# First norm of the decoder trunk: x is turned unscaled, the root of the mean square is multiplied in later, and x and the first weight tiles load on two queues

## The chip, the cores and the metric

The kernel runs on one core of a Trainium2 chip. The metric is device time in microseconds (us) of one execution; lower is better. The engines named below are TensorE (PE; PEld is its weight load), VectorE (DVE), ScalarE (ACT), GpSimd (POOL) and SyncE (SP). SP issues nearly all DMAs; ACT can issue DMAs too, from its own instruction stream.

## The reference

A trunk of two layers over 256 tokens of width 1024, in fp32. Only the first sub-layer is touched:

```
def rms_norm(x, g):
    y = x * rsqrt(mean(x * x, axis=-1) + 1e-6)
    return y * g
...
def short_conv_mixer(h, w_in, conv_w, w_out):
    b_gate, c_gate, z = split(h @ w_in, 3, axis=-1)      # w_in is 1024 x 3072
    u = c_gate * z
    u_conv = causal depthwise convolution of u, width 3
    return (b_gate * u_conv) @ w_out
...
x = x + short_conv_mixer(rms_norm(x, norm_mix[0]), conv_w_in, conv_w, conv_w_out)
x = x + peer_ffn(rms_norm(x, norm_ffn[0]), ...)          # then attention, and a second peer_ffn
```

The root of the mean square is one number per token. It multiplies all three parts of `h @ w_in`, so it can be applied to a product instead of to x.

## The kernel before

All products run on TensorE as three products of two parts each (a high part and a rest): high weight by high x, low weight by high x, high weight by low x. Weights come as a stream of numbered **items** of 128 x 1024 fp32 (512 KB). Items 0 to 23 are `conv_w_in` (four DMAs of 128 KB each), items 24 to 31 `conv_w_out`, then the peer layer follows. Three buffers `raw`, `hi`, `lo` go round, so item n uses buffer n mod 3.

- `split_to(n)` (L162 on): ACT copies `raw` to `hi` (L171), then DVE or POOL computes `lo = raw - hi` (L176). Items 0, 1, 2 and 25 of this layer have their `lo` on POOL (`on_pool`), the others on DVE. Item 0's `lo` is made in two halves (`halved`).
- `issue()` (L129 on) issues the DMAs of item n+3 as soon as item n is split.
- `next_item(mm, budget)` emits the split of item n+2, then the products of item n, then calls `run_side(budget)`, which emits queued side work (`add(cost, f)`) until the budget is spent; `pause` ends a round. So the order in which each engine works is the order in which the Python code emits; every engine takes its instructions strictly in that order.
- `mm_wstat(banks, b)` (L472): one item of `conv_w_in`, 24 products of 128 x 256. Items 0 to 7 go to the PSUM banks `lo4` (the c gate), 8 to 15 to `hi4` (z), 16 to 23 to `lo4` again (the b gate). I call these the first, second and third group.
- `norm_in()` computes the first norm: squares on ACT (L334), the root in small DVE steps (`begun`, `mean`, `root`), a multiplication by root and gain (`scaled`, L367), turning by TensorE (`turned`, L372) and splitting into high part `XH` (L377) and rest `XL` (L382). The gain row is spread over the partitions by TensorE (`spread_gain`, L276).
- After the first group ACT copies `lo4` to `cT` (L583). In the third group, DVE and ACT compute the convolution as side work: u (L588, DVE), first tap (L592, ACT), two more taps (L594, DVE). After item 23, DVE multiplies the b gate by the convolution (L610) and the result is split into `XH` and `XL` (L611, L605) for `conv_w_out`.
- Before all that, `warm(n)` issues n products on the identity to raise the granted clock, and `preload()` has ACT load its table.

Of the kernel before, what the change touches and what calls it, by code (L numbers as in the profile page):

```python
# [22 lines left out]
D = 1024  # L23
# [15 lines left out]
def trunk_kernel(ctx: ExitStack, tc, x, norm_mix, norm_ffn, conv_w_in, conv_w, conv_w_out,  # L39
# [89 lines left out]
    def issue():  # L129
        while state["dma"] < NI and released(state["dma"] - 3):  # L130
# [15 lines left out]
            elif isinstance(items[n][1], list):  # L146
                for q in (0, 2, 1, 3):
                    sp.dma_start(r[32 * q:32 * q + 32], items[n][1][q])
            else:
                sp.dma_start(r, items[n][1])  # L150
# [11 lines left out]
    def split_to(n):  # L162
        while state["split"] <= min(n, NI - 1):
# [6 lines left out]
            else:  # L170
                act.activation(HI[m % 3], src, AF.Copy)  # L171
# [88 lines left out]
    def load_x(i, h):  # L260
        c = slice(h * 512, h * 512 + 512)
        sp.dma_start(x_in[:, i * D + h * 512:i * D + h * 512 + 512], x[0, i * 128:(i + 1) * 128, c])
# [10 lines left out]
    def spread_gain(gb):  # L273

        for h in range(2):
            pe.matmul(gb[h], half_row, GN[0:1].rearrange("p (q c j) -> p c q j", q=4, j=32)[:, 4 * h:4 * h + 4],  # L276
                      start=True, stop=True)

    for i in range(2):
        for h in range(2):  # L280
            load_x(i, h)
        if i == 0:
            sp.dma_start(GN[0:1], norm_mix[0:1])
# [8 lines left out]
    half_row = scratch(0, 128)[0:1]  # L292
    dve.memset(half_row, -0.5)
# [7 lines left out]
    warm(WARM)  # L301
    spread_gain(hi4[2:4])
# [21 lines left out]
    def residual(bank, i, h):  # L324

        v = XT[i].rearrange("p (c q j) -> p c q j", q=4, j=32)[:, :, 2 * h:2 * h + 2]
        if bank is None:
            bank = x_in[:, i * D + h * 512:i * D + h * 512 + 512]
            dve.tensor_copy(v, bank.rearrange("p (q c j) -> p c q j", q=2, j=32))
            v = bank  # L330
        else:
            dve.tensor_tensor(v, bank.rearrange("p (q c j) -> p c q j", q=2, j=32), v, op=OP.add)
            v = XT[i].rearrange("p (c r) -> p c r", r=128)[:, :, 64 * h:64 * h + 64]
        act.activation(junk[:, 0:512] if len(v.shape) == 2 else junk[:, 0:512].rearrange("p (c r) -> p c r", r=64),  # L334
                       v, AF.Square, accum_out=ssq[:, 2 * i + h:2 * i + h + 1])
# [16 lines left out]
    def rms(banks):  # L352
        bk = banks or [None] * 4
        residual(bk[0], 0, 0)
        begun(0)
        residual(bk[1], 0, 1)
        mean(0)
        residual(bk[2], 1, 0)
# [26 lines left out]

    def norm_in():

        scaled, turned, first, parted = norm_parts(hi4, hi4[2:4])
# [854 lines left out]
```

## Time and profile before

| | us |
|---|---|
| median of 3 runs | 1823.19 (1821.16 to 1823.33) |
| the profiled execution | 1822.49 |
| its span | 1820.7 |
| TensorE busy in the span | 1797.7 |

The span is the time from the first to the last instruction on the core in the profile; the execution's own time has 1.8 us around it. A stretch in which TensorE has no gap can only become shorter by fewer products.

### The profile page before, as it was taken

The page shows a single profiled execution, that of the slowest core. Times are in us where ns is not written, and L with a number is a line of the kernel's source. Part 1 is how long each engine was busy: PE and PEld are TensorE (multiplying, and loading weights), DVE is VectorE, ACT ScalarE, POOL GpSimd, SP SyncE. Part 2 cuts the span into 40 slices and gives each one's busy share as a digit, 9 for nine tenths or more (in the row PEclk, how much of TensorE's full clock was granted, in tenths as well). Part 3 has the DMA queues.
Part 4 walks back from the last instruction along what each step waited for, and adds up shares of the span by engine and source line. Part 5 has one row for each costly group of instructions (what it writes and reads, how often), then busy time and mean ns, then how long its engine had stood idle before and what let it go on. Part 6 is the DMA issues. An engine that isn't in the chain of part 4 may idle for free.

```text
span 1820.7 us, 32357 instructions
## 1 busy us (share of the span) xinstructions
PE 1797.7 (99%) x11985; PEld 1573.6 (86%) x11985; DVE 1353.9 (74%) x2183; ACT 894.6 (49%) x1109; POOL 710.7 (39%) x549
## 2 busy tenths in 40 slices
PE   9999999999999999999999999999999999999998
PEld 8979999988888888888788799999888888888886
DVE  4748888788888887555567487887888898875555
ACT  5455445555454444544454554545455544445443
POOL 1048899978820000000200388999888300000000
PEclk9999999999999999999999999999999999999999
DMA  7566655665555555655562675556565555556564
GB/s 210 154 194 188 183 163 168 175 178 168 172 161 183 166 173 183 227 193 194 163 184 86 174 205 169 166 169 183 165 172 167 160 185 174 174 174 228 191 194 138
DMA packets 204581, 321.15 MB, mean 176 GB/s; under 512 B 26221, under 2 KB 157317, under 8 KB 203910
## 3 DMA queue, kind: packets, MB, share of 16 engines
q1 hardware_dynamic: 202006, 312.33, 56.2%
q10 hardware_dynamic: 2416, 6.75, 1.1%
q8 instruction: 94, 1.54, 0.4%
q14 instruction: 65, 0.53, 0.1%
HBM read 315.83 MB, written 3.15 MB: 175 GB/s over the span
## 4 chain that ended last, share of the span: by engine, by line
PE 90%; DVE 4%; DMA 2%; ACT 1%; POOL 1%; issue 1%; SPq 0%; DVEq 0%; ACTq 0%; POOLq 0%
PE psum L485 41%; PE psum L878 13%; PE psum L884 12%; PE psum L880 5%; PE psum L881 5%; PE psum L1085 3%; PE psum L472 3%; PE psum L518 2%; DVE big L215 1%; POOL lo L176 1%; DVE tr L157 1%; PE psum L916 1%; DVE lo L176 1%; DMA raw<-in_conv_w_out_dram 1%; ACT hi L171 1%
## 5 line engine op out<-in xcount | busy, mean ns | idle before, releaser
L176 POOL TENSOR_TENSOR lo<-tr,hi 128x512 fp32r<-128x512 f32 x496 | 652.3, 1348 | 109.4 <-ACT hi L171 104.8
L176 DVE TENSOR_TENSOR lo<-raw,hi 128x1024 fp32r<-128x1024 f32 x316 | 388.1, 1229 | 259.1 <-ACT hi L171 253.1
L171 ACT ACTIVATE hi<-raw 128x1024 fp32r<-128x1024 f32 x331 | 349.7, 1060 | 448.4 <-PE psum L485 365.4
L485 PE MATMUL psum<-hi,x 128*128 128x512 f32 x2208 | 553.0, 392 | 0.7 <-ACT hi L171 0.7
L485 PEld LDWEIGHTS psum<-hi,x 128*128 128x128 f32 x2208 | 409.0, 188 | 82.6 <-ACT hi L171 1.1
L157 DVE STREAM_TRANSPOSE tr<-raw 128x1024 f32<-128x1024 f32 x256 | 316.0, 1234 | 64.2 <-POOL lo L176 38.2
L171 ACT ACTIVATE hi<-tr 128x1024 fp32r<-128x1024 f32 x256 | 270.3, 1058 | 128.4 <-DVE tr L157 113.5
L884 PE MATMUL psum<-x,lo 128*128 128x256 f32 x2048 | 292.0, 283 | 6.2 <-POOL lo L176 6.2
L485 PE MATMUL psum<-lo,x 128*128 128x512 f32 x1104 | 295.2, 389 | 0.4 <-POOL lo L176 0.4
L884 PEld LDWEIGHTS psum<-x,lo 128*128 128x128 f32 x2048 | 273.6, 191 | 18.6 <-POOL lo L176 8.6
L176 POOL TENSOR_TENSOR lo<-raw,hi 128x512 fp32r<-128x512 f32 (+1 forms) x27 | 49.1, 1848 | 609.5 <-ACT hi L171 557.3
L878 PE MATMUL psum<-x,hi 128*128 128x512 f32 x1024 | 263.6, 398 | 0.0
L880 PE MATMUL psum<-x,hi 128*128 128x256 f32 x1024 | 252.7, 284 | 0.8 <-ACT hi L171 0.8
L881 PE MATMUL psum<-x,hi 128*128 128x256 f32 x1024 | 251.1, 283 | 0.0
L485 PEld LDWEIGHTS psum<-lo,x 128*128 128x128 f32 x1104 | 207.1, 188 | 43.9 <-POOL lo L176 0.8
L878 PEld LDWEIGHTS psum<-x,hi 128*128 128x128 f32 x1024 | 183.6, 189 | 33.3
L880 PEld LDWEIGHTS psum<-x,hi 128*128 128x128 f32 x1024 | 196.3, 192 | 1.5 <-ACT hi L171 1.2
L881 PEld LDWEIGHTS psum<-x,hi 128*128 128x128 f32 x1024 | 196.4, 192 | 0.2
L1185 POOL TENSOR_TENSOR big<-xbuf,big 128x256 f32<-128x256 f32 x2 | 1.4, 732 | 383.4 <-DVE rstd L348 383.4
L1070 DVE TENSOR_TENSOR xbuf<-psum,eT 128x1536 f16<-128x1536 f16 x128 | 119.9, 937 | 10.1 <-PE psum L1085 10.1
L1040 ACT ACTIVATE big<-psum 128x512 f32<-128x512 f32 x64 | 38.2, 597 | 125.6 <-PE psum L884 125.6
L1022 ACT ACTIVATE big<-psum 128x512 f32<-128x512 f32 x64 | 38.1, 596 | 115.6 <-PE psum L884 115.5
(164 smaller groups left out, 1573.4 us busy)
## 6 DMA issues: line engine op xcount, KB each, us to landing
raw<-in_peer_u_dram SPq DMA_DIRECT2D x1024, 128.0 KB, 3.0
raw<-in_peer_v_dram SPq DMA_DIRECT2D x256, 512.0 KB, 4.2
raw<-in_conv_w_in_dram SPq DMA_DIRECT2D x96, 128.0 KB, 2.6
raw<-in_attn_w_qkv_dram SPq DMA_DIRECT2D x96, 128.0 KB, 2.7
raw<-in_peer_w_q_dram SPq DMA_DIRECT2D x64, 128.0 KB, 2.9
raw<-in_conv_w_out_dram SPq DMA_DIRECT2D x8, 512.0 KB, 4.2
raw<-in_attn_w_o_dram SPq DMA_DIRECT2D x8, 512.0 KB, 3.7
x_dram<-xbuf ACTq DMA_DIRECT2D x2, 1024.0 KB, 4.8
```

Source lines behind the costliest of these rows:

```text
L157: dve.transpose(TR[m % 3].rearrange("p b (g i) -> p g b i", g=4), RAW[m % 3].rearrange("p (g m) -> p g m", m=256))
L171: act.activation(HI[m % 3], src, AF.Copy)
L176: eng.tensor_sub(LO[m % 3][:, c], src[:, c], HI[m % 3][:, c])
L472: pe.matmul(banks[c // 2][:, (c % 2) * 256:(c % 2) * 256 + 256], w[:, c * 128:c * 128 + 128], xx[:, b], start=(b == 0 and p == 0 and c % 2 ...
L485: pe.matmul(banks[j], x[:, j // 2 * 128:j // 2 * 128 + 128], w[:, j % 2 * 512:j % 2 * 512 + 512], start=(first and p == 0), stop=(last and ...
L878: pe.matmul(o, w, X2[:, b], start=(b == 0), stop=False, skip_group_check=True)
L880: pe.matmul(o, w, XH[:, b], start=(b == 0), stop=False)
L881: pe.matmul(o, w, XL[:, b], start=False, stop=False)
L884: pe.matmul(o[:, 0:256], lo[:, b * 128:b * 128 + 128], XH[:, b], start=False, stop=(b == 7), skip_group_check=(o.shape[-1] == 512))
L1040: act.activation(A[:, k - 1:k + 1], halves(k, 1), AF.Copy)
L1070: dve.tensor_tensor(HOT[s % 2].rearrange("p b (r k) t -> p b r k t", r=3), numbers[:, None, None].to_broadcast([128, TOK // 2, 3, 64, 2]), ...
L1085: pe.matmul(o, pairs[:, t // 2, :, t % 2], OHG[s % 2][:, a, t // 2, :, t % 2], start=(a == 0), stop=(a == 1))
```

## The change

The order of the work in the first sub-layer, not its result, is changed:

- x is loaded in other halves (128 columns of each quarter, so 512 bytes in a row where it was 2 KB): the first halves on ACT's queue, the second on SP's. Item 1's four DMAs go on ACT's queue too. The norm weight comes as 8 rows of 128 and is turned by TensorE into `gT`, one column per chunk.
- x is put in order by DVE (`kept`), turned as it is by TensorE and multiplied by the gain as it is split (`chunk`: ACT writes `XH`, DVE `XL`), chunk by chunk; chunks 0 to 3 ahead of item 0's products, 4 to 7 after item 1's.
- Item 0's `hi` is made in two halves, and its products run in the order high-high, high-low, low-high. Only item 0 is split ahead (before: items 0 and 1).
- Squares, mean and root become side work of items 2 to 4. `factors(i)` puts the root on a diagonal and TensorE multiplies it by ones, after items 4 and 5; `row` makes from that `R` (the root, minus one half included, in a row for all partitions) and `R2` (its square).
- `cT` is made by DVE as `lo4` times `R2` (before: copied by ACT). In the third group u and the first taps (`gate`) are queued one step ahead of the other taps (`taps`), and each pair of chunks is multiplied by `R` (`normed`, new).
- The loads of the second norm's gain and of the peer keys on ACT's queue move from before item 0's products into the second group.

The diff, cut to its core:

```
+    gr8 = scratch(7 * D + 128, 128)[0:8]
+    sp.dma_start(gr8.rearrange("c (q j) -> c q j", q=4), norm_mix[0].rearrange("(q c j) -> c q j", q=4, j=32))
     for i in range(2):
-        for h in range(2):
-            load_x(i, h)
-        if i == 0:
-            sp.dma_start(GN[0:1], norm_mix[0:1])
+        load_x(act, i, 0)
+    issue(1)
+    for i in range(2):
+        load_x(sp, i, 1)
     issue()
...
+    def chunk(c):
+        bk = hi4[c // 2][:, c % 2 * 256:c % 2 * 256 + 256]
+        for i in range(2):
+            pe.transpose(bk[:, i * 128:i * 128 + 128], XT[i][:, c * 128:c * 128 + 128], ident)
+        act.activation(XH[:, c], bk, AF.Copy, scale=gT[:, c:c + 1])
+        dve.scalar_tensor_tensor(XL[:, c], bk, gT[:, c:c + 1], XH[:, c], op0=OP.mult, op1=OP.subtract)
...
     def norm_in():
...
+        for i in range(2):
+            kept(i, 0)
+        chunk(0)
         split_to(0)
+        for c in (1, 2, 3):
+            chunk(c)
+        warm(2)
+        def factors(i):
+            dg = scratch(i * 128, 128)
+            dve.tensor_scalar(dg, ident, rstd[:, i:i + 1], -0.5, op0=OP.mult, op1=OP.mult)
+            pe.matmul(hi4[0][:, i * 128:i * 128 + 128], ones, dg, start=True, stop=True)
+        def row():
+            dve.tensor_copy(R, hi4[0][:, 0:256])
+            dve.tensor_tensor(R2, R, hi4[0][:, 0:256], op=OP.mult)
+        pause(2)
+        for i in range(2):
+            for h in range(2):
+                add(0.3, squares, i, h)
+            add(0.2, begun, i)
+            add(0.2, mean, i)
+        pause()
+        for i in range(2):
+            add(0.6, root, i)
+            add(0.2, factors, i)
+        pause()
+        add(0.6, row)
...
-            next_item(mm_wstat(lo4, b), 1.0)
+            next_item(mm_wstat(lo4, b), 1.5)
+            if b == 0:
+                for i in range(2):
+                    kept(i, 1)
+            if b == 1:
+                for c in range(4, 8):
+                    chunk(c)
...
-                    act.activation(uc[:, c], uT[:, c, 0:256], AF.Copy, scale=cwT[:, 0, c:c + 1])
-                    for k in (1, 2):
-                        dve.scalar_tensor_tensor(uc[:, c], uT[:, c, k:k + 256], cwT[:, k, c:c + 1], uc[:, c],
-                                                 op0=OP.mult, op1=OP.add)
-                add(0.9, f)
+        def normed(j):
+            s = slice(2 * j, 2 * j + 2)
+            dve.tensor_tensor(uc[:, s], uc[:, s], R[:, None].to_broadcast([128, 2, 256]), op=OP.mult)
+        add(0.6, gate, 0)
+        for j in range(4):
+            if j < 3:
+                add(0.6, gate, j + 1)
+            for k in (1, 2):
+                add(0.9, taps, j, k)
+            add(0.6, normed, j)
...
-            next_item(mm_wstat(lo4, b), 2.4, b < 7)
+            next_item(mm_wstat(lo4, b), 2.5, b < 7)
```

Three places show how the engines' orders move. Lines of the changed kernel are numbered anew: L171 becomes L173, L176 L178, L472 L486, L588 L615, L592 L617, L594 L621, L610 L648.

The first place is the start of the program on ACT, in the changed kernel; a wait named DMAHW is one for an earlier DMA (DMAHW0 is that of x's first part, DMAHW2 that of item 0's first quarter).

```order
L265 DMA big<-in_x_dram 128x4x128 x2
L148 DMA raw_67<-in_conv_w_in_dram 32x1024 x2
L148 DMA raw_67<-in_conv_w_in_dram 32x1024 [waits DMAHW0_49]
L148 DMA raw_67<-in_conv_w_in_dram 32x1024 [waits DMAHW2_49]
L255 ACT_TABLE_LOAD
L255 ACTIVATE idle<-one 128x1 [waits DVE_49]
L256 ACTIVATE idle<-one 128x1 [waits Activation_49]
L387 ACTIVATE x_78<-psum,gT 128x256 [waits PE_49]
L173 ACTIVATE hi_72<-raw_66 128x512 [waits DMAHW7_49,DMAHW5_49,DMAHW1_49]
L173 ACTIVATE hi_72<-raw_66 128x512
```

Before, the table load was ACT's first instruction; now six DMA issues stand ahead of it, two of which wait for landings.

On POOL the same place reads, in the changed kernel:

```order
L178 TENSOR_TENSOR lo_75<-raw_66,hi_72 128x512 x2
L314 IOTA iota_t 128x128
L590 MEMSET big 128x8x2
L178 TENSOR_TENSOR lo_76<-raw_67,hi_73 128x1024
L178 TENSOR_TENSOR lo_77<-raw_68,hi_74 128x1024
```

Before, the iota and the memset (L312, L576) stood behind the `lo` of item 1; now they stand ahead of it.

The second place is the end of item 4 on PE in the changed kernel (item 4 uses hi_73 and lo_76, item 5 hi_74); L416 is the product in `factors`.

```order
L486 MATMUL psum<-x_78,lo_76 128x256 [waits DVE_49]
L486 MATMUL psum<-x_78,lo_76 128x256 x7
L486 MATMUL psum<-x_78,hi_73 128x256 x8
L416 MATMUL psum<-big 128x128 [waits DVE_49]
L486 MATMUL psum<-x_78,hi_74 128x256 [waits Activation_49]
L486 MATMUL psum<-x_78,hi_74 128x256 x7
```

What it waits for on DVE (L415, behind the split of item 6, which is lo_75 here):

```order
L178 TENSOR_TENSOR lo_77<-raw_68,hi_74 128x1024
L335 TENSOR_SCALAR part<-ssq 128x1
L339 TENSOR_SCALAR var<-ssq,part 128x1
L178 TENSOR_TENSOR lo_75<-raw_66,hi_72 128x1024
L345 RECIPROCAL rstd<-newt 128x1
L346 TENSOR_SCALAR newt<-rstd,var 128x1
L347 TENSOR_SCALAR rstd<-newt,rstd 128x1
L415 TENSOR_SCALAR big<-ident,rstd 128x128
```

Before, nothing stood between items 4 and 5 on PE; now a product does that needs the `lo` of item 6 and the root.

The third place is the third group on DVE, from the split of item 18 on: first before, then in the changed kernel (L626 is `normed`).

```order
L176 TENSOR_TENSOR lo_75<-raw_66,hi_72 128x1024
L588 TENSOR_TENSOR big<-big,psum 128x2x256
L594 SCALAR_TENSOR_TENSOR big<-big,cwT 128x256 x2
L176 TENSOR_TENSOR lo_76<-raw_67,hi_73 128x1024
L594 SCALAR_TENSOR_TENSOR big<-big,cwT 128x256 x2
L588 TENSOR_TENSOR big<-big,psum 128x2x256
L594 SCALAR_TENSOR_TENSOR big<-big,cwT 128x256 x2
L176 TENSOR_TENSOR lo_77<-raw_68,hi_74 128x1024
```

```order
L178 TENSOR_TENSOR lo_75<-raw_66,hi_72 128x1024
L615 TENSOR_TENSOR big<-big,psum 128x2x256 x2
L621 SCALAR_TENSOR_TENSOR big<-big,cwT 128x256 x2
L178 TENSOR_TENSOR lo_76<-raw_67,hi_73 128x1024
L621 SCALAR_TENSOR_TENSOR big<-big,cwT 128x256 x2
L626 TENSOR_TENSOR big<-big 128x512
L615 TENSOR_TENSOR big<-big,psum 128x2x256
L178 TENSOR_TENSOR lo_77<-raw_68,hi_74 128x1024
L621 SCALAR_TENSOR_TENSOR big<-big,cwT 128x256 x4
L626 TENSOR_TENSOR big<-big 128x512
L615 TENSOR_TENSOR big<-big,psum 128x2x256
L178 TENSOR_TENSOR lo_75<-raw_66,hi_72 128x1024
```

Before, each L588 had two taps between it and the next split; now each L615 of items 19 on stands right ahead of a split. On ACT the two first taps that follow from an L615 (L617) stand ahead of the `hi` of the next item in every round; before, one of the two stood ahead of it and the other behind.

## Rows read from the trace of the kernel before

**Rows 1.** The page: busy time by engine; chain that ended last, by engine.

```profile
PE 1797.7 (99%) x11985; PEld 1573.6 (86%) x11985; DVE 1353.9 (74%) x2183; ACT 894.6 (49%) x1109; POOL 710.7 (39%) x549
...
PE 90%; DVE 4%; DMA 2%; ACT 1%; POOL 1%; issue 1%; SPq 0%; DVEq 0%; ACTq 0%; POOLq 0%
```

**Rows 2.** Chain of waits up to 150 us: start us, us, what.

```profile
1.19 0.42 SPq L262
...
2.02 4.46 DMA big<-in_x_dram
...
12.22 3.14 PE psum L472 x24
15.36 0.87 PE psum L372 x8
...
19.27 40.52 PE psum L472 x336
...
85.75 1.06 ACT hi L171
```

**Rows 3.** Timeline, 0 to 30 us: start us, us, engine, line, operation, [idle before].

```profile
0.74 1.28 ACT L253 ACT_TABLE_LOAD   x1 [0.74 <-PEq L1230]
...
2.04 0.20 ACT L253 ACTIVATE idle<-one 128x1 f32<-128x1 f32 x1
...
3.80 0.43 DVE L329 COPY xbuf<-big 128x512 f32<-128x512 f32 x1 [2.34 <-DMA big<-in_x_dram]
...
10.97 4.89 POOL L176 TENSOR_TENSOR lo<-raw,hi 128x512 fp32r<-128x512 f32 x3 [9.90 <-DMA raw<-in_conv_w_in_dram]
...
15.81 0.84 POOL L312 IOTA iota_t<- 128x128 f16 x1
...
16.67 2.41 POOL L176 TENSOR_TENSOR lo<-raw,hi 128x1024 fp32r<-128x1024 f32 x1
```

**Rows 4.** Stretches: PE, PEld, DVE, ACT, POOL busy us, granted clock, DMA share, GB/s.

```profile
6.00:8.00 2.00, 1.24 (x3) 0.18 (x1) 1.58 (x5) 1.14 (x3) 0.00 (x0) 0.91 1.05 284
8.00:10.00 2.00, 1.80 (x9) 1.49 (x10) 1.62 (x7) 1.15 (x5) 0.00 (x0) 0.50 1.04 283
...
36.00:48.00 12.00, 12.00 (x103) 12.00 (x102) 5.11 (x5) 5.32 (x6) 0.00 (x0) 1.00 0.62 192
...
78.00:84.00 6.00, 5.96 (x47) 5.62 (x46) 5.92 (x10) 2.52 (x4) 0.00 (x0) 1.00 0.67 201
```

**Rows 5.** Groups by line and shape up to 125 us: busy us, mean ns | idle before.

```profile
L171 ACT ACTIVATE hi<-raw 128x1024 fp32r<-128x1024 f32 x38 | 39.6, 1054 | 34.7 <-PE psum L472 19.4 <-DMA raw<-in_conv_w_out_dram 7.1 <-DMA raw<-in_conv_w_in_dram 5.3
L176 DVE TENSOR_TENSOR lo<-raw,hi 128x1024 fp32r<-128x1024 f32 x30 | 37.9, 1270 | 34.8 <-ACT hi L171 32.3 <-DMA raw<-in_conv_w_in_dram 2.1 <-PE psum L485 0.3
...
L594 DVE SCALAR_TENSOR_TENSOR big<-big,cwT 128x256 f32<-128x256 f32 x16 | 7.7, 484 | 2.6 <-ACT big L592 2.3
...
L334 ACT ACTIVATE big<-big 128x512 f32<-128x512 f32 x4 | 2.5, 630 | 2.5 <-DMA big<-in_x_dram 2.4
...
L276 PE MATMUL psum<-big 1*128 1x512 f32 x4 | 2.0, 613 | 0.0
```

**Rows 6.** Timelines of ACT and of DVE in the third group.

```profile
59.81 1.06 ACT L171 ACTIVATE hi<-raw 128x1024 fp32r<-128x1024 f32 x1 [1.82 <-PE psum L472]
62.76 0.51 ACT L592 ACTIVATE big<-big,cwT 128x256 f32<-128x256 f32 x1 [1.89 <-DVE big L588]
63.18 1.04 ACT L171 ACTIVATE hi<-raw 128x1024 fp32r<-128x1024 f32 x1
...
60.90 1.23 DVE L176 TENSOR_TENSOR lo<-raw,hi 128x1024 fp32r<-128x1024 f32 x1 [1.65 <-ACT hi L171]
62.05 0.68 DVE L588 TENSOR_TENSOR big<-big,psum 128x512 f32<-128x512 f32 x1
63.30 1.01 DVE L594 SCALAR_TENSOR_TENSOR big<-big,cwT 128x256 f32<-128x256 f32 x2 [0.58 <-ACT big L592]
...
81.39 1.31 DVE L610 TENSOR_TENSOR psum<-big,psum 128x512 f32<-128x512 f32 x2
```

More of the change, by code (lines that the diff above doesn't have):

```diff
@@ L127, in released, with issue @@
         return n < 0 or n < state["split"] or (is_u(n) and n < state["tr"])
-    def issue():
-        while state["dma"] < NI and released(state["dma"] - 3):
+    def issue(end=NI):
+        while state["dma"] < end and released(state["dma"] - 3):
             n = state["dma"]
@@ L170, in split_to @@
             else:
-                act.activation(HI[m % 3], src, AF.Copy)
+                for c in (range(0, 1024, 512) if m == 0 else (0,)):
+                    w = slice(c, c + (512 if m == 0 else 1024))
+                    act.activation(HI[m % 3][:, w], src[:, w], AF.Copy)
             eng = pool if (is_u(m) or m in on_pool) and m not in on_dve else dve
@@ L291, in trunk_kernel @@
     dve.tensor_scalar(ident, jp, 0.0, None, op0=OP.is_equal)
-    half_row = scratch(0, 128)[0:1]
-    dve.memset(half_row, -0.5)
+    ones = scratch(256, 128)
+    dve.memset(ones, 1.0)
     i16 = ident.bitcast(BF16)
@@ L299, in warm @@
             pe.matmul(B[0][:, 0:256], i16[:, 0:128], i16, start=True, stop=True)
-    warm(WARM)
-    spread_gain(hi4[2:4])
+    warm(WARM - 8)
+    gT = sb.tile([128, 8], F32, name="gT")
+    pe.transpose(lo4[3][:, 0:8], gr8, ident[0:8, 0:8])
+    dve.tensor_copy(gT, lo4[3][:, 0:8])
+    warm(6)
     def load_keys(l):
@@ L469, in f @@
                 order = [(c, p) for c in range(8) for p in range(3)]
+            elif b == 0:
+                order = [(c, p) for p in (0, 2, 1) for c in range(8)]
             for c, p in order:
@@ L576, in conv_mixer @@
         pool.memset(uT[:, :, 0:2], 0.0)
-        load_gain(norm_ffn, 0)
-        load_keys(0)
         for b in range(8):
-            next_item(mm_wstat(lo4, b), 1.0)
+            next_item(mm_wstat(lo4, b), 1.5)
[5 more added lines that the diff above has]
+                    chunk(c)
         drain_side()
-        for j in range(4):
-            act.activation(cT[:, 2 * j:2 * j + 2].rearrange("p c t -> p (c t)"), lo4[j], AF.Copy)
@@ new lines, in conv_mixer, with gate, taps @@
+        pause()
+        add(0.0, load_gain, norm_ffn, 0)
+        add(0.0, load_keys, 0)
+        for b in range(8):
+            next_item(mm_wstat(hi4, b), 1.5)
+        drain_side()
+        def gate(j):
+            s = slice(2 * j, 2 * j + 2)
+            dve.tensor_mul(uT[:, s, 2:258], cT[:, s], hi4[j].rearrange("p (c t) -> p c t", t=256))
+            for c in range(2 * j, 2 * j + 2):
+                act.activation(uc[:, c], uT[:, c, 0:256], AF.Copy, scale=cwT[:, 0, c:c + 1])
+        def taps(j, k):
+            for c in range(2 * j, 2 * j + 2):
+                dve.scalar_tensor_tensor(uc[:, c], uT[:, c, k:k + 256], cwT[:, k, c:c + 1], uc[:, c],
+                                         op0=OP.mult, op1=OP.add)
```

81 lines of the change are left out of this document (24 added, 57 removed).

## The prediction

> **What bounds the kernel now.** I read the page first: TensorE is busy 99% of the span, and 90% of the chain that ended last is its own [rows 1]. So an edit counts only where TensorE waits, or where the chain leaves it. The chain of waits shows three such places in the first 90 us [rows 2]. At the start the chain is the DMA of x, until 6.48; the first product of item 0 stands at 12.22. From 19.27 the 336 products of items 2 to 15 run in 40.52 us, 0.12 us each, **2.88 us an item**, with no gap worth naming. In the third group it leaves TensorE again: the `hi` of item 18 starts at 59.81, and the chain goes over ACT and DVE to the first multiplication by the convolution (L610) at 81.39 [rows 6], with DVE busy 5.92 of the last 6 us [rows 4]. After it the `hi` of item 25 starts at 85.75 [rows 2], and the items that follow wait for buffers, one behind the other. There is no lead anywhere in three buffers, so I take what is gained or lost at L610 as gained or lost at the end. The sum is therefore a new time for L610: 81.39 plus or minus what each part does.
>
> **Part 1, the front.** Removed ahead of item 0: the squares, the root and the multiplication. What is left is x's landing, one turn, two ACT copies. ACT now issues six DMAs before its table load. SP's first issue stood at 0.74 and its landing freed a DVE copy at 3.80 [rows 3]; ACT's first is the same transfer in size, so its third issue for item 1, which waits for that landing, goes at about 3.8, the fourth at 4.2 (0.42 each [rows 2]), and the queue is free at 4.6. The table load is 1.28 and the two dummy activations start right behind it [rows 3], 0.4 in all: ACT is free at 6.3. Chunk 0 takes about 0.47 (nearest row: 128 x 256 with a scale per row, 0.51, and 0.42 from start to start [rows 6]). Item 0's `hi` needs all of item 0: with the first halves of x and half of item 1 sent between, 1.25 MB must come. Of the 3.06 us from SP's first issue to that copy, 256 KB at the 283 GB/s of a saturated stretch [rows 4] are 0.9 and 2.1 is fixed; 1.25 MB are 4.6, so the tile is there at 0.74 + 2.1 + 4.6 = 7.5. Half a `hi` is 0.6 (1.05 for the whole [rows 5]): **first product at 8.2, 4.0 earlier.** Bounds: if the 512-byte pieces of x go at half the rate, 512 KB cost 1.9 more (10.1); if ACT is free earlier and the tile lands at 6.8, 7.4.
>
> The Trainium skill (ScalarE: Activation LUTs, What ACT_TABLE_LOAD costs) puts a drain of 1.38 us behind a table load, which would free ACT at 7.7 and put the first product at 8.9, the sum at +6.1. The dummy activation starts 0.02 us after the load here [rows 3], so the trace does not show that drain.
>
> The two queues themselves I cost at nothing: the DMA engines are at a share of 1.04 to 1.05 from 6 to 10 us [rows 4], so the total of 2.5 MB arrives no earlier. The Trainium skill (DMA: Bandwidth & Descriptors, Issuing engines are not separate DMA queues) says the same against this part of the change: two issuers save issue time only. If the queues did add up, item 0 would land by 5 and ACT alone would hold the first product, at 7.4: a total of 0.8 less (1827.8).
>
> The granted clock was 0.50 from 8 to 10 us [rows 4], after TensorE had idled; I expect that again under item 0. It is hidden by the wait in part 2 as long as it adds less than 1.9; were all 32 products there at half speed, they would cost 3.8 more, 1.9 net. DVE's copies of x (0.43 each [rows 3]) and the rests of the chunks run while TensorE works on the high parts or waits for POOL; without that cover each rest would add some 0.45.
>
> **Part 2, POOL.** Three `lo` in a row take 4.89: two halves of 1.27 and one of 2.4; the iota with its memset holds POOL 0.86 (15.81 to 16.67) [rows 3]. Both now stand ahead of item 1's `lo`: 8.1 + 2.5 + 0.9 + 2.4 = 13.95. TensorE reaches that point at 12.0 (32 products from 8.2) and waits 1.9; the 16 products left and eight turns (0.87 [rows 2]) put item 2 at 16.9, **2.4 ahead of 19.27.** 1.6 of the gain is lost here. The DMA is not what is waited for: 2.5 MB are 9.3, so item 2 lands near 0.74 + 2.1 + 9.3 = 12.1. If the iota ran before the halves, the gain would be 3.2.
>
> **Part 3, the root as side work.** The product in `factors(0)` stands on PE between items 4 and 5, and its operand on DVE behind the `lo` of item 6. I followed that back from item 1's end at 15.95: first turns 0.5; four chunk copies on ACT 1.7; `hi` 4 0.95; two squares 1.5 (0.63 each [rows 5], and the reading of the sum); a root on ACT that waits for the mean, behind `lo` 4, 0.45; a third square 0.75; `hi` 5 1.05; `lo` 5 1.25; the second mean and root 0.6; `hi` 6 1.05; `lo` 6 1.25; three root steps and the diagonal 0.95. Together 12.0, less 0.3 of overlap between neighbours: ready at 27.6. TensorE has done item 4 at 16.9 + 3 x 2.88 = 25.5, so it **waits 2.1**. With the product itself (0.25; 512 fp32 columns are 1.0 [rows 5]) item 5 starts at 27.8. Before it was 19.27 + 8.64 = 27.9. So 2.3 more of the gain is gone. The chain starts from item 1's end, so an earlier start moves both alike. Bounds: 0.5 (if only `lo` 6 and the root were late) and 3.0.
>
> The second factor comes when item 5 is done and costs 0.25, and the turn of the convolution weights, which stood ahead of item 2, now costs its 0.17 at item 7: 0.4. **Item 16 starts 0.3 later than before.** The four multiplications of `cT` on DVE (0.68 each, as L588 [rows 6]) lie in a group where DVE is busy 5.1 of 12 us [rows 4], as do the moved loads, at a DMA share of 0.62; without that cover they would cost 2.7 and up to 1.3.
>
> **Part 4, the third group.** New work: four `normed`, 128 x 512 from SBUF. The trace has 128 x 1024 at 1.23 [rows 5], so 0.62. That alone is 2.5 us on an engine that has almost no gap. The order costs as much again. Each `hi` stands on ACT behind two first taps, these wait for the L615 at the very end of DVE's round, and DVE's next instruction is the `lo` that needs this `hi`. So DVE idles for two taps and a `hi`, 0.84 + 1.05, once a round. Before, two taps on DVE (1.01) lay in that gap, and it was 0.58 [rows 6].
>
> From the start of `hi` 18: `hi` 1.1, `lo` 1.15, first L615 0.7, four taps on ACT 1.7, `hi` 19 1.05 (5.7); `lo` 1.2, two taps 0.95, `normed` 0.58, L615 0.65, two ACT taps 0.9, `hi` 20 1.05 (11.0); `lo` 1.2, four taps 1.85, `normed` and L615 1.25, ACT 0.9, `hi` 21 1.05 (17.25); `lo` 1.2, four taps and `normed` 2.4; `lo` 22 1.15, 2.4 again; `lo` 23 and 24 2.3: first multiplication at **26.7**. Before: 81.39 - 59.81 = 21.6. **5.1 later.** TensorE feels it first at item 21. Item 18 starts 2 x 2.88 after 59.79, 4.7 after its `hi` is done at 60.87 [rows 6]; so `hi` 21 is due 8.64 + 4.7 after that and comes 16.15 after it: a wait near 3. Bounds: 2.5, if the gaps fill and only `normed` counts; 6.
>
> **Sum.** -4.0 (front) + 1.6 (POOL) + 2.3 (root) + 0.4 (moved products) + 5.1 (third group) = **+5.4**. The profiled execution took 1822.49 (its span 1820.7 and 1.8 around it), so 1827.9 for it; the median stands 0.7 above it, and for the median I say **1828.6**.
>
> **The rivals.**
> 1. *The root is in time.* If DVE and ACT overlap better between items 2 and 5 than I add up, the wait of 2.1 shrinks to 0.5 and the third group costs 4 to 5. Result 5.4 - 1.6 = +3.8 down to +2, 1825 to 1827. For it: a dozen summands, each with some overlap. Against: each of them waits for the one before, or stands behind it on its engine.
> 2. *The third group hides its work* (the other side): the chain from `hi` 18 to the first multiplication stays at 21.6, because u is begun for two pairs of chunks at once and the lead absorbs the rest. Then the front decides: -4.0 + 1.6 + 2.3 + 0.4 = +0.3, and with the root's wait at 0.5 and a first product at 7.4, -2.1, with the iota's 0.9 hidden -3.0: 1820 to 1823.5. Faster by more than 3.65 needs 0.65 beyond all that. It holds if the new work of 5.1 fits into the 4.7 us that `hi` 18 leads its use by. Against: DVE's 5.92 of 6 [rows 4].
> 3. *The front is slow.* Small pieces of x at half the rate, or a low clock through item 1: +1.9 to +2.6 on the sum, 1830.5 to 1831.5. For it: x's DMA is the first link of the chain already [rows 2]; no row shows pieces of 512 bytes.
>
> **How the numbers follow.** Forecast (+3.8 to +7.3) 0.62, rival 1 0.18, rival 2 0.08, rival 3 0.12. A measurement of this kernel can tell about 0.2%, 3.65 us. Slower: forecast and rival 3, 0.74. The same: rival 1 and most of rival 2, 0.23. Faster: the rest of rival 2, 0.03. The range leaves out rival 2 and the far ends of 1 and 3: 1824.5 to 1832.
>
> **What would show it.** Part 1: the first L486 near 8.2 and the table load near 4.6. Part 2: L486 waits for POOL once, near 12 to 14. Part 3: L416 waits for DVE about 2 us, near 25.5. Part 4: L178 on DVE waits for ACT, 1.5 to 2.1 in each of three rounds; L486 waits about 3 for the `hi` of item 21; the first L648 near 81.39 + 5.4 = 86.8. If L486 has no wait between items 4 and 5 and none at 21, I am wrong, and the time is below 1824.

## The result and the profile after

The changed kernel takes **1831.99 us** (median of 4, 1831.83 to 1834.27); the kernel before took 1822.47 beside it (1821.16 to 1823.33). The ratio is 1.0056 [1.0038, 1.0073]: slower, as forecast, but by 9.5 us where 5.4 were worked out; the upper end of the stated range, 1832, lay 8.8 above the 1823.19 that it was worked out from, and 9.5 is more. The profiled execution took 1831.83, its span 1830.0.

The page of the changed kernel, the two rows that answer to [rows 1]:

```profile
PE 1798.2 (98%) x11978; PEld 1575.0 (86%) x11978; DVE 1359.3 (74%) x2196; ACT 893.6 (49%) x1110; POOL 710.8 (39%) x549
...
PE 89%; DVE 4%; DMA 3%; ACT 2%; POOL 1%; issue 1%; SPq 0%; DVEq 0%; ACTq 0%; POOLq 0%
```

TensorE's busy time has hardly moved (1797.7 to 1798.2) while the span grew by 9.3. So what was lost is idle time of TensorE. The chain of waits (start us, us, what; the stretches of [rows 2]) says where:

```profile
2.84 5.93 DMA raw<-in_conv_w_in_dram
...
10.34 0.89 DVE x L388 x2
11.27 0.69 PE psum L386 x2
12.38 6.78 PE psum L486 x48
19.43 0.48 ACT x L387
19.93 0.49 DVE x L388
...
32.89 0.49 PE psum L416 x2
33.38 2.87 PE psum L486 x24
...
65.66 1.07 ACT hi L173
...
96.17 1.06 ACT hi L173
```

Before, the chain lay on TensorE from 19.27 with 336 products in one piece. Now it leaves TensorE for L388 (DVE's rest of a chunk) ahead of item 0 and again between items 1 and 2, and for the root at 32.89 (L416, the product in `factors`). TensorE's own timeline shows the same places as waits, in brackets:

```profile
8.40 1.11 PE L386 MATMUL psum<-ident,xbuf 128*128 128x128 f32 x4 [1.08 <-DVE x L388]
11.27 0.69 PE L386 MATMUL psum<-ident,xbuf 128*128 128x128 f32 x2 [1.75 <-DVE x L388]
...
12.04 3.29 PE L486 MATMUL psum<-x,hi 128*128 128x256 f32 x16
...
20.47 0.66 PE L386 MATMUL psum<-ident,xbuf 128*128 128x128 f32 x4 [1.09 <-DVE x L388]
22.39 0.44 PE L386 MATMUL psum<-ident,xbuf 128*128 128x128 f32 x2 [1.26 <-DVE x L388]
22.58 1.20 PE L486 MATMUL psum<-x,hi 128*128 128x256 f32 x8
...
32.89 0.49 PE L416 MATMUL psum<-big 128*128 128x128 f32 x2 [1.44 <-DVE big L415]
```

L386 is a chunk's turn. Chunks 2j and 2j + 1 are turned into the two halves of one bank (`hi4[c // 2]`), and the turn of the second waits until ACT and DVE have read the first. The trace puts each of these waits down to L388; the run with the banks apart, below, shows that the shared bank is the cause.

ACT's rows show a second thing about the front that the extracts ahead of the prediction leave out:

```profile
8.79 1.15 ACT L173 ACTIVATE hi<-raw 128x512 fp32r<-128x512 f32 x2 [0.96 <-DMA raw<-in_conv_w_in_dram]
9.85 0.82 ACT L387 ACTIVATE x<-psum,gT 128x256 fp32r<-128x256 f32 x2
```

ACT works strictly in order, and the split of item 0 (L173) stands between its copies (L387) of chunk 0 and of chunks 1 and 2. So ACT waits 0.96 for item 0's tile, and chunks 1 and 2 are copied only behind the split, though the turn of chunk 3, ahead of item 0's products, needs chunk 2 read out of the bank that both share: that is its wait of 1.75. The chain ahead of item 0 is thus the tile's landing, two half splits, two copies, DVE's rest of a chunk, a turn, and then the first product at 12.04.

In stretches (the columns of [rows 4]):

```profile
6.00:8.00 2.00, 0.33 (x1) 0.14 (x1) 0.56 (x2) 1.71 (x4) 0.00 (x0) 0.95 1.03 236
8.00:10.00 2.00, 1.11 (x4) 0.71 (x4) 0.35 (x1) 1.21 (x3) 0.50 (x1) 0.50 1.12 251
10.00:12.00 2.00, 0.73 (x4) 0.61 (x5) 0.88 (x2) 0.67 (x3) 2.00 (x3) 0.50 1.07 280
12.00:14.00 2.00, 2.00 (x11) 2.00 (x10) 1.15 (x3) 2.00 (x3) 1.35 (x3) 0.50 0.64 195
...
78.00:84.00 6.00, 3.39 (x24) 3.18 (x24) 4.05 (x8) 3.26 (x5) 0.00 (x0) 0.91 0.30 87
```

The granted clock is 0.50 (the lower of its two levels, 1.2 GHz of 2.4) from 8 to 14 us, and item 0's 16 first products take 3.29 us; at the 0.12 each of [rows 2] they would take 1.9. And the DMA engines, at the same full share as in [rows 4], move 236 and 251 GB/s where it was 284 and 283.

The third group (ACT's `hi` of item 18, then DVE, then TensorE), which answers to [rows 6]:

```profile
65.66 1.06 ACT L173 ACTIVATE hi<-raw 128x1024 fp32r<-128x1024 f32 x1 [1.35 <-PE psum L486]
...
71.31 1.23 DVE L178 TENSOR_TENSOR lo<-raw,hi 128x1024 fp32r<-128x1024 f32 x1 [1.26 <-DMA raw<-in_conv_w_in_dram]
...
76.57 1.23 DVE L178 TENSOR_TENSOR lo<-raw,hi 128x1024 fp32r<-128x1024 f32 x1 [1.92 <-ACT hi L173]
77.72 1.67 DVE L621 SCALAR_TENSOR_TENSOR big<-big,cwT 128x256 f32<-128x256 f32 x4
79.41 0.69 DVE L626 TENSOR_TENSOR big<-big 128x512 f32<-128x512 f32 x1
...
82.62 1.23 DVE L178 TENSOR_TENSOR lo<-raw,hi 128x1024 fp32r<-128x1024 f32 x1 [1.92 <-ACT hi L173]
...
91.79 1.32 DVE L648 TENSOR_TENSOR psum<-big,psum 128x512 f32<-128x512 f32 x2
```

```profile
82.64 1.89 PE L486 MATMUL psum<-x,hi 128*128 128x256 f32 x8 [2.61 <-ACT hi L173]
```

Put side by side, the terms of the sum as differences from the kernel before, between the same points of the program (from these rows and [rows 2, 6]; item 5 starts at 33.14 after, at 27.91 before):

| stretch | predicted | measured |
|---|---|---|
| up to item 0's first product (12.22 before, 12.04 after) | -4.0 | -0.2 |
| from there to item 2 (19.27, 22.58) | +1.6 | +3.5 |
| item 2 to item 5 | +2.3 | +1.9 |
| item 5 to `hi` 18 (59.81, 65.66) | +0.4 | +0.6 |
| `hi` 18 to the first multiplication (81.39, 91.79) | +5.1 | +4.6 |
| behind it | 0 | -1.1 |
| sum | +5.4 | +9.3 |

The three terms from item 2 to the first multiplication are close. The first two are where the prediction failed: together -2.4 was forecast and +3.3 came. The table is that of one execution each; two runs below whose front is the same have `hi` 18 at 66.49 and 67.67 in place of 65.66, so its middle terms are good to a microsecond or two.

The multiplication came 10.4 later and the end only 9.3. Part of that comes back by item 31: the `hi` of item 28 is 10.3 later than before (93.19, 103.49), that of item 31 9.7 (99.94, 109.60), whose tile landed 3.65 after its wait began where it was 4.30. The rest is open.

### The profile page after: what moved, and what is told of

Same layout as the page of the kernel before. It is cut to its first block, busy times and chain, and to the rows that moved or that the text cites. A ratio compares the mean times of both kernels' runs of the same rounds, so it can differ in the third digit from the quotient of the medians.

```text
span 1830.0 us, 32355 instructions
## 1 busy us (share of the span) xinstructions
PE 1798.2 (98%) x11978; PEld 1575.0 (86%) x11978; DVE 1359.3 (74%) x2196; ACT 893.6 (49%) x1110; POOL 710.8 (39%) x549
## 4 chain that ended last, share of the span: by engine, by line
PE 89%; DVE 4%; DMA 3%; ACT 2%; POOL 1%; issue 1%; SPq 0%; DVEq 0%; ACTq 0%; POOLq 0%
PE psum L499 40%; PE psum L916 13%; PE psum L922 12%; PE psum L918 5%; PE psum L919 5%; PE psum L1123 3%; PE psum L486 2%; PE psum L532 2%; DVE big L217 1%; POOL lo L178 1%; DMA raw<-in_conv_w_in_dram 1%; ACT hi L173 1%; DVE lo L178 1%; DVE tr L157 1%; PE psum L954 1%
## 5 line engine op out<-in xcount | busy, mean ns | idle before, releaser
L178 POOL TENSOR_TENSOR lo<-tr,hi 128x512 fp32r<-128x512 f32 x496 | 652.3, 1349 | 109.1 <-ACT hi L173 106.0
L178 DVE TENSOR_TENSOR lo<-raw,hi 128x1024 fp32r<-128x1024 f32 x316 | 389.4, 1233 | 260.1 <-ACT hi L173 248.9
L173 ACT ACTIVATE hi<-raw 128x1024 fp32r<-128x1024 f32 (+1 forms) x332 | 349.6, 1057 | 451.2 <-PE psum L499 365.4
L173 ACT ACTIVATE hi<-tr 128x1024 fp32r<-128x1024 f32 x256 | 270.4, 1058 | 127.4 <-DVE tr L157 115.8
L178 POOL TENSOR_TENSOR lo<-raw,hi 128x512 fp32r<-128x512 f32 (+1 forms) x27 | 49.1, 1843 | 618.9 <-ACT hi L173 576.7
```

The source lines that it names most:

```text
L173: act.activation(HI[m % 3][:, w], src[:, w], AF.Copy)
L178: eng.tensor_sub(LO[m % 3][:, c], src[:, c], HI[m % 3][:, c])
```

## The experiments

All times are medians; ratios are to the kernel before, timed on the same chip.

**The banks.** One edit: chunk c goes to bank c % 4, so that two chunks that follow each other never share one.

```
-        bk = hi4[c // 2][:, c % 2 * 256:c % 2 * 256 + 256]
+        bk = hi4[c % 4][:, c // 4 * 256:c // 4 * 256 + 256]
```

> The changed kernel with each chunk turned into a PSUM bank of its own (chunk c in bank c mod 4), nothing else. Theory A (TensorE waits for VectorE only because two chunks share a bank): the turns of chunks 1 and 3 no longer wait, the first product of item 0 comes at about 9.4 us instead of 11.96, the turns between items 1 and 2 take about 1 us instead of 3.6, item 5 starts about 4 us earlier than 33.14, and the time falls by about 4 us, to 1828. Theory B (the front is late because of the landing of item 0 and the lower clock): first product still at 11 to 12 us, the time within 1 us of 1832.

Measured: 1830.99, ratio 1.0047 [1.003, 1.0064]. TensorE's timeline:

```profile
9.61 2.22 PE L486 MATMUL psum<-x,hi 128*128 128x256 f32 x16 [1.33 <-ACT hi L173]
...
15.60 1.22 PE L486 MATMUL psum<-x,lo 128*128 128x256 f32 x8 [1.65 <-POOL lo L178]
...
17.62 1.04 PE L386 MATMUL psum<-ident,xbuf 128*128 128x128 f32 x8
18.41 1.20 PE L486 MATMUL psum<-x,hi 128*128 128x256 f32 x8
...
30.33 0.49 PE L416 MATMUL psum<-big 128*128 128x128 f32 x2 [3.05 <-DVE big L415]
```

The mechanism is shown: every wait for L388 is gone, the turns of chunks 4 to 7 take 1.04 in place of 3.6, and item 2 starts 4.2 earlier. But only 1.0 of it reaches `hi` 18 (64.62) and the first multiplication (90.75). Of the 4.2, 1.6 go at the root: its chain does not come forward as far, so L416 now waits 3.05 in place of 1.44. Another 1.3 go behind that wait, where the products of item 5 run slow (24 in 4.2 us in place of 2.9). The medians differ by 1.0 too, but by themselves they would not show it, since the intervals of the two ratios overlap.

**The third group.** Two runs, each with the changed front. The first puts the group back in the order of before (u, two chunks of taps, then `normed`; the budget of a round back to 2.4), with `normed` on DVE; the second leaves the new order and moves `normed` to POOL.

```
-        add(0.6, gate, 0)
...
+            add(0.6, mul, j)
+            for c in (2 * j, 2 * j + 1):
+                add(0.9, f, c)
+            add(0.0, normed, j)
```

```
-            dve.tensor_tensor(uc[:, s], uc[:, s], R[:, None]
+            pool.tensor_tensor(uc[:, s], uc[:, s], R[:, None]
```

> The changed kernel with the third group in the order of before (one multiplication, then three taps per chunk), and the multiplication by the root kept, after each pair of chunks. Theory A (half of the 4.5 us that the third group lost is work, half is order): from the hi of item 18 to the first multiplication by the b gate 24.0 us instead of 26.1, the time 1.5 to 2 us lower. Theory B (all of it is the new work on VectorE): 26 us, no change.

> The changed kernel with the four multiplications by the root on GpSimd, which is idle in the third group; the order stays. Theory A (work and order each half): 26.1 falls by the 2.4 us of four multiplications, to about 23.7, and the gaps of 1.9 us ahead of lo on VectorE stay. Theory B (all is work): 26.1 falls to 21.6, and the gaps go. Theory C (all is order): no change.

Measured: 1831.43 for both, ratios 1.0052 [1.0035, 1.0068] and 1.0049 [1.0032, 1.0065]. From `hi` 18 to the first multiplication it is 25.1 in the old order (the last 0.58 of it a wait for TensorE) and 24.3 with POOL, against 26.1 as changed and 21.6 before. So order and new work both cost, but the end moved by only 0.6 in each, within what single medians of this kernel can tell. In both profiles the front came later than in that of the changed kernel (`hi` 18 at 66.49 and 67.67 in place of 65.66) and ate up most of the gain: the first multiplication stands at 91.62 and 91.93, where it was 91.79. TensorE's rows give the cause: behind the two waits for a bank (1.08 and 1.26) item 2 ran slow, 4.1 and 4.4 us in place of 2.9, with the clock at 0.78 and 0.58 from 24 to 28 us, where the changed kernel's own profile has 1.00. POOL's rows show why the second takes less off this stretch than its 4 x 0.69 us of DVE:

```profile
80.73 1.29 POOL L626 TENSOR_TENSOR big<-big 128x512 f32<-128x512 f32 x1 [4.03 <-DVE big L621]
86.06 2.21 POOL L626 TENSOR_TENSOR big<-big 128x512 f32<-128x512 f32 x1 [4.04 <-DVE big L621]
89.82 3.35 POOL L626 TENSOR_TENSOR big<-big 128x512 f32<-128x512 f32 x1 [1.55 <-DVE big L621]
```

Where DVE idles beside it, POOL's multiplication takes 1.29; where DVE works from SBUF beside it, 2.21 and 3.35, and DVE's four taps take 2.70 in place of 1.66.

**All three together.**

> All three edits together: banks of their own, the third group in the order of before, the multiplication by the root on GpSimd. If the causes add up: -4 for the banks and -4.5 for the third group, 1823 to 1824, so within 0.1% of the kernel before; what stays is the wait at the product of the root, near 2 us. If something else of the change costs time (the moved loads, the lower clock), 1826 or more.

Measured: 1827.92, ratio 1.0032 [1.0019, 1.0044]. Alone the three gave 1.0, 0.6 and 0.6; together 4.1. In this profile `hi` 18 stands at 65.72, as in the changed kernel (65.66), so what the banks free is lost again ahead of it; from there to the first multiplication it is 22.7 in place of 26.1, so 3.4 of the 4.1 come from the third group. What is left is the root: the wait at L416 is 3.33, and the stretches behind it have the clock at 0.65 and 0.50:

```profile
28.00:32.00 4.00, 1.46 (x7) 1.46 (x8) 3.51 (x9) 1.22 (x2) 0.00 (x0) 0.65 0.68 207
32.00:36.00 4.00, 4.00 (x20) 4.00 (x20) 0.53 (x2) 0.00 (x0) 0.00 (x0) 0.50 0.55 162
```

**The wait filled.** On top of all three, 28 products that nobody reads (bfloat16, 128 x 256), ahead of the first root product.

```
+            if i == 0:
+                for _ in range(28):
+                    pe.matmul(hi4[1][:, 0:256], i16[:, 0:128], i16, start=True, stop=True)
             pe.matmul(hi4[0][:, i * 128:i * 128 + 128], ones, dg, start=True, stop=True)
```

> All three edits together (banks, the third group's old order, POOL for the multiplication), and 28 products of 128x256 in bfloat16 into a bank that holds nothing, on TensorE ahead of the first root product, so that TensorE is not idle while it waits (they add nothing to the output). If idling brings the low granted clock, the root product stays near 30.5 to 30.9, but item 5's 24 products take 2.9 in place of 4.98, and the time falls by 1.5 to 2.1, to 1826 to 1826.5. Rival: the low clock comes from something else (the load of the other engines), then item 5 stays slow and the time at 1827.9 or above.

Measured: 1826.3, ratio 1.0021 [1.0012, 1.003], 1.6 less than without the filling:

```profile
26.97 3.23 PE L418 MATMUL psum<-ident 128*128 128x256 bf16 x28
...
30.52 1.20 PE L489 MATMUL psum<-x,hi 128*128 128x256 f32 x8
31.56 1.12 PE L489 MATMUL psum<-x,lo 128*128 128x256 f32 x8
32.52 1.12 PE L489 MATMUL psum<-x,hi 128*128 128x256 f32 x8
```

Item 5 still starts at 30.5, but its 24 products now take 2.9 (5.2 without the filling) and the clock is 1.00; `hi` 18 comes at 63.05 in place of 65.72. So the idling cost its own 3.3 us and more behind it: 1.6 by the medians, 2.7 between the two profiles.

**The root late.** On top of all three: the diagonal is made right behind its root, and both root products and the row copy stand behind item 6.

```
         for i in range(2):
-            add(0.6, root, i)
-            add(0.2, factors, i)
+            add(0.5, root, i)
+            add(0.2, diagonal, i)
         pause()
+        pause()
+        for i in range(2):
+            add(0.2, factors, i)
         add(0.6, row)
```

> All three edits of the run before, and the two root products with the row copy behind item 6 (each diagonal is made on DVE right behind its root). Theory: the wait of 3.3 us at the root product and the low granted clock that follows it (24 products of item 5 in 4.98 us instead of 2.9) are what the freed banks ran into. Then TensorE has no wait between items 4 and 5, no low clock there, hi 18 starts near 61 (65.7 before this edit), and the time falls by 4 to 5, to 1823 to 1824. Rival: the second parts of items 5 and 6 are as late as the root is, so that a wait of 1 to 2 stays at item 5 or 6, and the time is 1825.5 to 1827.

Measured: 1822.83, ratio 1.0003 [0.9994, 1.0012]; 5.1 less. The root products have no wait, and nothing behind them runs slow:

```profile
32.27 1.12 PE L492 MATMUL psum<-x,hi 128*128 128x256 f32 x8
33.23 0.61 PE L419 MATMUL psum<-big 128*128 128x128 f32 x4
```

`hi` 18 starts at 60.14, so of the 5.9 us that it was late (65.66 and 59.81) 5.5 are gone by the banks and the root, without a change of the products.

**The root alone.** The same edit on the changed kernel, with shared banks and the changed third group.

> The changed kernel with the diagonals right behind their roots and both root products and the row copy behind item 6, and nothing else. Theory: alone this takes away only the wait of 1.44 at the root product that the changed kernel shows, and no low clock, since none follows it there: item 5 starts at 31.2 to 31.7 (33.2), the time falls by 1.5 to 2, to 1830 to 1830.5, though the same edit on top of freed banks took 5.1. Rival: it takes 4 to 5 here as well, to 1827 to 1828.

Measured: 1832.77 (1830.3 to 1833.47), ratio 1.0051 [1.0037, 1.0065]: no gain clear of noise. The expectation was not met in that; the wait of 1.44 is gone, yet:

```profile
22.00 0.66 PE L386 MATMUL psum<-ident,xbuf 128*128 128x128 f32 x4 [1.08 <-DVE x L388]
23.92 0.44 PE L386 MATMUL psum<-ident,xbuf 128*128 128x128 f32 x2 [1.26 <-DVE x L388]
24.11 1.95 PE L492 MATMUL psum<-x,hi 128*128 128x256 f32 x8
...
24.00:28.00 4.00, 4.00 (x22) 4.00 (x23) 1.99 (x4) 3.26 (x8) 0.00 (x0) 0.57 0.03 8
```

In this execution the low clock follows the bank waits (0.57 granted from 24 to 28), and item 2 needs 4.4 us, as it did in the two profiles of the third group; in the changed kernel's own it did not. The five times fall into two groups, 1830.3 and 1830.7, and 1832.8 to 1833.5: the lower two are what the expectation says. That the low clock parts the two groups is not shown, since only one of the five was profiled.

**The gaps filled.** The run with the root alone, and nine unread products ahead of the turns of chunks 5 and 7.

```
                 for c in range(4, 8):
+                    if c % 2:
+                        for _ in range(9):
+                            pe.matmul(hi4[0][:, 0:256], i16[:, 0:128], i16, start=True, stop=True)
                     chunk(c)
```

> The run with the root's products alone moved, and nine idle products of 128x256 in bfloat16 (into a bank that is done with) on TensorE ahead of the turns of chunks 5 and 7, where it waited for DVE 1.08 and 1.26 us. The bank waits themselves stay. Theory: in that run the root's wait was gone, but item 2 and the start of item 3 ran at a low granted clock behind these gaps (24 products in 4.4 us in place of 2.9), which ate the gain; filled, item 2 takes 2.9, and the time falls by 1.3 to 1.8, to 1830.8 to 1831.5. Rival: the low clock stays whatever fills the gaps (it comes from the wait ahead of item 0), and the time stays at 1832.5 or above.

Measured: 1831.27 (1830.38 to 1831.8), ratio 1.0047 [1.0033, 1.006], 1.5 less; items 2 to 5 follow each other at 2.88 with the clock at 1.00. That bears the theory out but does not prove it: the intervals of the two ratios overlap, and two of the five times without the filling were as low. By the profiles, item 2 ran slow in three of the four with the waits unfilled, and at full pace in the one with them filled. So the waits for a bank cost their length, and in some executions the pace of the next item too.

**POOL's iota behind.** On top of the run with the root late, the iota and the memset move behind the `lo` of item 2.

```
-        late_consts()
-        pool.memset(uT[:, :, 0:2], 0.0)
         for b in range(8):
             next_item(mm_wstat(lo4, b), 1.5)
             if b == 0:
+                late_consts()
+                pool.memset(uT[:, :, 0:2], 0.0)
```

> As the one with the root late, and iota and memset on POOL behind the lo of item 2 in place of ahead of item 1's. Theory of the prediction's part 2: TensorE's wait for POOL at item 1 (1.65) loses the 0.9 that iota and memset hold POOL, item 2 starts 0.9 earlier, at 17.5, and the time falls by 0.9, to 1822 to 1823. Rival: the transfers hold the items behind it (hi 4 waited 1.1 to 1.3 for its tile), so that a wait of about 0.9 turns up at item 3 or 4, and the time is that of the kernel with the root late.

Measured: 1821.99, ratio 1.0 [0.9991, 1.0009]; 0.8 less, item 2 at 17.68. The term of 0.9 for the iota in part 2 is shown.

**The root as a scale of tokens.** On top of that, `normed` is left out; a token's root is multiplied in where the output product is added to x, which has tokens on partitions. The result is the same sum in another order.

```
-            pool.tensor_tensor(uc[:, s], uc[:, s], R[:, None].to_broadcast([128, 2, 256]), op=OP.mult)
...
+            for q in range(2):
+                dve.scalar_tensor_tensor(v[:, :, q], bv[:, :, q], fac[:, i:i + 1], v[:, :, q], op0=OP.mult, op1=OP.add)
```

> As the one with iota behind, without the multiplication of the convolution's output by the root (four instructions): the root of each token is multiplied in where the bank of the output product is added to x, in the instruction that adds (two of 128x256 for one of 128x512). Theory: the new work of the third group is then nothing, the chain from hi 18 to the first multiplication by the convolution is 21.6 as in the kernel before (22.7 with POOL), the additions cost 0.1 to 0.3, and with item 16 1 to 1.5 earlier than in the kernel before the time is 1821 to 1822, at or just below it. Rival: POOL's multiplications were hidden already and what is left of the group comes from DVE's order, then no change against the kernel with iota behind.

Measured: 1821.16, ratio 0.9995 [0.9986, 1.0004]. From `hi` 18 (59.07) to the first multiplication (80.63) it is 21.56, as before. Each addition takes 0.88 for the pair in place of 0.69 (0.19 more, four times).

**Item 1's transfers behind.** On top of that, item 1's four DMAs go on SP's queue behind item 0's, so that ACT's queue carries only x.

```
-                    (act if n == 1 else sp).dma_start(r[32 * q:32 * q + 32], items[n][1][q])
+                    sp.dma_start(r[32 * q:32 * q + 32], items[n][1][q])
...
-    issue(1)
+    issue(2)
```

> As the kernel with the token scale, and the four transfers of item 1 on SP's queue behind those of item 0 (and ahead of the second halves of x), so that ACT's queue carries only the first halves of x. Theory: the second queue is not free; the pieces of item 1 share the DMA engines with those of item 0 and make it land about 1 us later than the sum of the prediction's part 1 (hi 0 at 9.03 here, 7.5 predicted). Then hi 0 starts near 7.7, the first product stands at 8.2 to 8.7 (9.72 without this edit), item 2 starts at 16 to 17 (17.7), and the time is 1819.5 to 1820.5. Rival: the rate of 512-byte pieces or the turns of chunks 1 to 3 set the first product, then it stays at 9.3 or later, and the time at 1821.

Measured: 1820.66, ratio 0.9989 [0.998, 0.9998].

ACT's split of item 0, with the edit and, in the last line, without it:

```profile
2.10 1.28 ACT L256 ACT_TABLE_LOAD   x1 [2.10 <-issue]
...
7.65 1.14 ACT L174 ACTIVATE hi<-raw 128x512 fp32r<-128x512 f32 x2
...
9.03 1.15 ACT L174 ACTIVATE hi<-raw 128x512 fp32r<-128x512 f32 x2 [1.07 <-DMA raw<-in_conv_w_in_dram]
```

The first product is at 8.33 (9.72 without the edit), with the same 512-byte pieces of x. The table load is earlier with the edit too, but without it ACT had been idle for 1.07 when the tile came, so the load did not hold it. What made item 0 late by these 1.4 was the second queue, with the pieces of x the same in both: item 1's tile took its share of the DMA engines while item 0's was on its way. The Trainium skill (DMA: Bandwidth & Descriptors, Issuing engines are not separate DMA queues) has all issuers end on the same 16 engines and interleave; the trace agrees, 259 GB/s from 4 to 6 us with one queue for the tiles and 261 with two. Item 2 keeps the 1.4 (it starts at 16.28, without the edit at 17.69), though item 1 waits 0.83 for POOL's `lo`. The median fell by only 0.5; against the kernel before, timed beside each, it is 1.29 below in the run without the edit and 2.11 with it. In the profiled execution, the slowest of eleven (1821.55), the lead is lost in the second group: the `hi` of item 15 waits 5.09 us for its tile (to 52.30; 2.53 without the edit), and `hi` 18 waits 0.94 for its own and starts at 58.77, only 0.3 earlier. From 48 to 52 us the DMA engines move 92 GB/s there. The loads of the second norm's gain and of the peer keys, which the change moved into this group, are issued from 43.27 to 44.67, just ahead of it. Whether they are the cause no run tests.

**Warmer.** On top of that, four more unread products ahead of chunk 0's turns.

```
-    warm(6)
+    warm(10)
```

> As the one with item 1's transfers behind, and four more idle products (10 in place of 6) ahead of chunk 0's turns, in the gap in which TensorE waits for the second tile of x. Theory: the 16 first products of item 0 took 3.5 to 3.8 us after such a gap and 2.64 in the run without one, so they fall to about 2.6; what of that reaches the end depends on POOL, whose lo of item 1 comes behind: 0 to 0.9 faster, 1819 to 1820. Rival: four products do not change the pace of item 0, no change.

Measured: 1819.96 (1819.51 to 1821.31), ratio 0.9987 [0.9978, 0.9996]. Item 0's 16 first products take 2.22 in this run and 2.21 in the one without the four, so the four more bring nothing there, as the rival said. The 0.7 between the two medians is not theirs, as far as the profiles go: this one's front is 0.27 later (item 2 at 16.55), but its `hi` 18 does not wait for a tile and starts at 57.94 in place of 58.77, and the first multiplication is 0.83 earlier (79.51, 80.34). So the two profiles differ by the transfers of the second group; whether the medians do is not shown. Nor does the gap ahead of these 16 products set their pace in an obvious way: it was 1.33 us in the run with the banks apart, where they took 2.22, and 0.42 in the run with the root late, where they took 3.78. This version has the lowest median, 2.8 us below the kernel before and 12 below the changed one.

## Why the prediction failed

**Part 1, the front: the step that failed.** "What is left is x's landing, one turn, two ACT copies" left out that chunks 1 to 3 stand on TensorE ahead of item 0's products and that each second one waits for its bank. The diff shows the line (`hi4[c // 2]`), but none of the places taken from the order is TensorE's own row ahead of item 0. It cost 2.4 us ahead of item 0 (12.04, and 9.61 with the banks apart). The table load came at 5.54 and not near 4.6, since ACT's fourth issue waited for x; but ACT then idled 0.96 for item 0's tile, so this did not hold the product. The Trainium skill (PSUM — Partial Sum Buffer, PSUM bank collisions raise a hardware error) has the rule that speaks against this part, and I did not weigh it: guard by bank and quadrant, or by bank in its simple version, and not by address. The waits in the trace fit that, as they end with the bank's last reader and are gone with the banks apart; the page gives no price for them, the runs do: 1.08 to 1.75 us each.

**Part 1, the two queues: "at nothing" was wrong** by 1.4 at the first product and at item 2; what of it reaches the end is not settled (0.5 to 1.1 between the medians, as one compares them). The rate of 283 GB/s was too high as well (236 to 259 from 2 to 8 us). With one queue the tile was there by 7.65, where 7.5 was worked out, and the first product stood at 8.33 with the banks apart, where 8.2 was.

**Part 2, POOL: the mechanism was right, and hidden.** The wait of 1.9 for item 1's `lo` was gone in the changed kernel, because item 0 came late; with the banks apart it was 1.65. The term that failed is the eight turns "(0.87)": a price from turns into free banks. They took 3.6.

**Part 3, the root: right in kind.** The wait was 1.44 where 2.1 was forecast, since TensorE itself was late; with the banks apart it was 3.05, as the chain from item 1's end (17.6) took 12.7 and not 11.7. What the sum did not have at all is what follows a wait of 3 us, in the runs with the banks apart: 1.3 to 2.1 us at the lower clock. In the changed kernel's own profile nothing slow follows the 1.44.

**Part 4, the third group: right.** 26.1 against 26.7; DVE's gaps were 1.26, 1.92 and 1.92 (1.5 to 2.1 forecast; the profile puts the first down to a DMA, but the `hi` of that item ends right there), TensorE's wait at item 21 2.61 (near 3). The runs with one half undone took 1.0 and 1.8 off, where the prediction priced order and work at some 2.5 each. The split between the two was off: in the old order the stretch is 21.56 without `normed`, 22.7 with it on POOL and 25.1 on DVE, so the work costs up to 3.6 (0.58 of it the wait for TensorE), and the new order 1.0 on top.

**The rivals.** Rivals 1 and 2 did not come. Rival 3 had the right direction and the wrong place: the clock was low under item 0 (48 products of items 0 and 1 in 6.97 us in place of 5.76), and the DMA engines moved fewer GB/s with the pieces of 512 bytes, but neither is the main cause.

The order of the causes can be read from the additions: banks 1.0 alone, root nothing clear of noise alone, yet banks, third group and root together 9.2 of the 9.5. The front of the changed kernel has two limits, the bank waits and the root, and where one goes the other holds. Still open is the larger part of the 1.1 that the changed kernel wins back behind the first multiplication, which executions meet the low clock at which gap, and what the loads moved into the second group cost.

## What to carry to other kernels

Before an edit is priced by the instructions that it adds, follow who writes and who reads each PSUM bank: two halves of one bank are one buffer, and the wait stands in front of everything queued behind it. The waits of 3.05 and 3.33 us on TensorE cost more than their length here, since the products behind them ran at the lower clock; unread products took that away, and a later place in the queue took the wait away as well. Undo causes together as well as one by one: here single edits gave 1.0, 0.6, 0.6 and 0, all within what a median of this kernel tells, and all of them together 9.2.

## What the hardware showed that I had not expected

- DVE and POOL slow each other when both work from SBUF: POOL's 128 x 512 multiplication 1.29 alone, up to 3.35 beside DVE; in the run with the token scale DVE's copy of x 0.43 alone and two of them 3.34 beside POOL's splits. The Trainium skill (SBUF — State Buffer, SBUF: two separate sides) names one port pair that both share and that one holds for a whole instruction; the rows agree. The page has this of VectorE in its two-port mode or with two inputs from SBUF, against a GpSimd operation that reads SBUF; a copy has one input, so only the first could hold for it, and no row shows the mode.

```profile
6.64 0.43 DVE L401 COPY xbuf<-big 128x512 f32<-128x512 f32 x1 [1.28 <-DMA big<-in_x_dram]
...
11.77 3.34 DVE L401 COPY xbuf<-big 128x512 f32<-128x512 f32 x2
```

- The lower clock came behind one wait of 3.05 or 3.33 us; behind two of 1.08 and 1.26 close together, in three profiles (the two of the third group, the root alone); and, in the changed kernel's own profile, behind the wait of 2.61 at item 21 (0.72 from 82 to 84, 0.50 from 84 to 86), where DVE holds the group anyway. It did not come behind the same 1.08 and 1.26, nor behind the 1.44, in that profile. So the length of one wait alone does not tell it.
- With x in 512-byte pieces the DMA engines at a share of 1.03 to 1.12 moved 236 and 251 GB/s from 6 to 10 us, with 2 KB pieces 283 and 284 at 1.04 and 1.05. That the size is the cause is not shown: other transfers share these stretches, and in the changed kernel they moved 280 at 1.07 from 10 to 12.
